# Inputs of a gated encoder layer laid out transposed by the host instead of turned on TensorE

## The chip, the cores and the metric

The kernel runs on one core of one Trainium2 chip. The metric is the device time of one execution in microseconds (us), as the median of repeated runs. The host's work on the inputs is not in it.

## The reference

One layer of an encoder works on x of 256 positions by 2048 channels in float32.

```python
def mixer_block(x, g_norm, w_in, ln_g, ln_b, w_s, b_s, rpb, w_branch, w_out):
    h = rms_norm(x, g_norm)
    proj = h @ w_in                    # 2048 -> 9216: u, v | q, k, v | two gates
    y_a = gmlp_branch(uv, ...)         # u * (W_s LN(gelu(v)) + b), 8 groups of 128 x 128
    y_b = neighbourhood_attn(q, k, v, rpb)
    merged = g_a * (y_a @ w_branch[:1024]) + g_b * (y_b @ w_branch[1024:])
    return x + merged @ w_out

def conv_ffn(x, g_norm, w_up, conv_k, conv_b, w_down):
    up = rms_norm(x, g_norm) @ w_up    # 2048 -> 11008
    ...                                # depthwise conv of width 3 over positions, plus conv_b
    return x + (silu(gate) * val) @ w_down
```

A last RMSNorm ends it. All weights are float32, and nearly all of the time is products with them.

## The kernel before

**Products in parts.** Each float32 operand is split into a high part (rounded, by a ScalarE copy) and a low part (the rest, by a VectorE subtraction), and a product is three matmuls: high by high, low by high, high by low (`triple`, L292 to L294). A matmul moves 512 columns.

**Pieces and groups.** Weights come in pieces of 512 KB: in the wide groups one piece is 128 rows (one k of the 2048-long sum) by 1024 columns. `load_to` issues the loads on SP's queue, up to five pieces ahead (five `wraw` buffers). `split_to` makes `whi` (ScalarE, L152) and `wlo` (VectorE, L153), in four buffers each. `begin(i)` opens piece i: it issues loads, runs the tasks that hand-written tables put at this piece (`at(i, f)`; `preload[i]` for loads that go on SP's queue just ahead of piece i), and splits later pieces. Every engine works through its own queue in this order. Pieces 0 to 15 are the V group (gMLP's v), 16 to 31 the VA group (attention's v), then come U (two groups of eight), q/k with the gates, and the rest.

A plain piece is twelve matmuls. Some pairs of pieces ("quads", at pieces 10 and 12 of V, and 20, 24, 28) save one of eight block products by sums: sums of blocks of x (`act_sums`, L306 and `act_blocks`, L298 to L301), of weights (`weight_sums`, L323 to L326), and splits of these (L313/L314, L333/L334). They need four banks of PSUM beside the four accumulators; there are eight banks.

**x and the vectors.** x is loaded by rows (positions on partitions) into `xs`, 256 columns at a time (`load_x`, 256 KB, L407). For each such chunk `x_chunk` turns four 128 x 128 blocks on TensorE (L510) into a PSUM bank; ScalarE and VectorE make the two parts from there, scaled by the norm vector `gmix` (L482, L489). `X_TURN` says at which piece: chunk 0 ahead of piece 0, chunk 3 at 1, chunks 1 and 4 at 2, 5 at 3, 2 at 4, 6 at 6, 7 at 9. The RMS factor is applied to the results: `x_stats` sums the squares of rows of `xs` on ScalarE (L1195, at pieces 7 to 14), and `x_norm` makes the factor (at 15).

The norm vectors and conv taps are loaded as rows of 128 values and turned on TensorE into columns (`vec_T`, L421, copied by VectorE at L422): `gmix` at the start, `gffn` and the four rows of taps and bias late, at pieces 33 to 35. The spatial weights are loaded into `ws_raw` and turned at pieces 31 and 32 (`turn_ws`, L1223, copied at L1224). TensorE's queue also has transposes of the identity that keep its clock up while the first loads are under way (`keep_awake`, L447): nine ahead of the turned `gmix`, eight after the first chunk of x.

Of the kernel before, what the change touches and what calls it, by code (L numbers as in the profile page):

```python
# [62 lines left out]
@with_exitstack  # L63
def trunk_kernel(ctx, tc, x, norm_mix, w_in, ln_g, ln_b, w_s, b_s, rpb, w_branch, w_out,
                 norm_ffn, w_up, conv_k, conv_b, w_down, norm_final, out):
    nc = tc.nc
# [22 lines left out]
    def bank():  # L89
        return psum.tile([128, 512], F32, name="bank")  # L90
# [19 lines left out]
    n_split = [0]  # L110
    first = {}

# [28 lines left out]
    def split_to(n):  # L141
        while n_split[0] < min(n, len(pieces)):
            i = n_split[0]
            n_split[0] += 1
            src, r0, kn, (c0, cn, nb, cs), step = pieces[i]
            w = raw.pop(i)
            h = wpool.tile([128, 2, 512], F32R, name="whi", bufs=SPLIT_AHEAD + 1)
            l = wpool.tile([128, 2, 512], F32R, name="wlo", bufs=SPLIT_AHEAD + 1)
            m = cn * nb

            def part(k):
                nc.scalar.activation(h[:, k, :m], w[:, k, :m], AF.Copy)  # L152
                nc.vector.tensor_sub(l[:, k, :m], w[:, k, :m], h[:, k, :m].bitcast(F32))  # L153
# [16 lines left out]
    def at(i, f):  # L170
        tasks.setdefault(i, []).append(f)
# [113 lines left out]

    def sum_acts_at(i, j, box, pair, room, name):
        at(i, lambda: act_sums(pair(), box, room))
        at(j, lambda: act_sums_split(box, room, name))
# [13 lines left out]

    def act_sums(a, box, room):
        w = room("f", F32)
        f = w[:, 0].rearrange("p (k t) -> p k t", k=2)
        nc.vector.tensor_add(f, a[:, :, 0, :].bitcast(F32), a[:, :, 1, :].bitcast(F32))  # L306
        act_blocks(w[:, 1], *(f[:, k, t * 128:(t + 1) * 128] for k in range(2) for t in range(2)))
        box["w"] = w
# [101 lines left out]
    def rows(src, off, n):  # L410
        return bass.AP(tensor=src.tensor, offset=src.offset + off, ap=[[128, n], [1, 128]])

    def vec_T(name, src, off, n, dst, queue=None):
        t = xin.tile([n, 128], F32, name=name)

        def load():
            (queue or nc.sync).dma_start(t, rows(src, off, n))

        def go():
            p = bank()  # L420
            nc.tensor.transpose(p[:, :n], t, ident[:n, :n])  # L421
            nc.vector.tensor_copy(dst, p[:, :n])  # L422
        return load, go

    gmix = const.tile([128, KD], F32)
    gffn = const.tile([128, KD], F32)
    ck = const.tile([128, 4, 2 * NF], F32)
    gm_load, gm_turn = vec_T("gm_rows", norm_mix, 0, KD, gmix, nc.scalar)
    gm_load()
    ws_raw = xin.tile([128, GMG, 128], F32)  # L430

    def load_ws():
        nc.sync.dma_start(ws_raw, bass.AP(tensor=w_s.tensor, offset=w_s.offset,
                                          ap=[[128, 128], [128 * 128, GMG], [1, 128]]))

# [12 lines left out]

    keep_awake(WAKE[0])
    late = [vec_T("gf_rows", norm_ffn, 0, KD, gffn)]  # L450
    for j in range(3):
        late.append(vec_T(f"ck_rows{j}", conv_k, j * 2 * DFF, 2 * NF, ck[:, j, :]))
    late.append(vec_T("cb_rows", conv_b, 0, 2 * NF, ck[:, 3, :]))


# [47 lines left out]
    x_pairs = [pair_of[hpool, f"h{c}"] for c in range(KD // 2)]  # L503

    def x_chunk(c):
        p = bank()
        for kk in range(2):
            k = c * 2 + kk
            for t in range(NT):
                nc.tensor.transpose(p[:, kk * T + t * 128:kk * T + (t + 1) * 128],  # L510
                                    xs[:, t, k * 128:(k + 1) * 128], ident)
        split_pair(p, xT[2 * c:2 * c + 2], gmix[:, 2 * c:2 * c + 2])

# [611 lines left out]
    for n, (q, i, j) in enumerate(X_SUMS):  # L1125
        sum_acts_at(i, j, first_sums[2 * q], lambda q=q: x_pairs[q],
                    lambda name, dt, i=i: first_room("s2" if name == "f" and i < 9 else name, dt), f"s{n}")
    g_u = [stationary(w_in2, 0, KD, U0 + j * 512, 512, 1, 0, xt, ev_u(j)) for j in range(2)]
# [73 lines left out]

    for n in range(8):
        at(STATS_AT + n, lambda n=n: x_stats(*divmod(n, 2)))
    at(NORM_AT, x_norm)
# [13 lines left out]

    def turn_ws(h):  # L1220
        p = bank()
        for g in range(4):
            nc.tensor.transpose(p[:, g * 128:(g + 1) * 128], ws_raw[:, h * 4 + g, :], ident)  # L1223
        nc.vector.tensor_copy(gm_pool["wsT"][:, h * 4:h * 4 + 4, :].rearrange("p a b -> p (a b)"), p)  # L1224
# [90 lines left out]
    def load_fin():  # L1315
# [12 lines left out]

_INS = ['x', 'norm_mix', 'w_in', 'gm_ln_g', 'gm_ln_b', 'gm_w_s', 'gm_b_s', 'na_rpb', 'w_branch', 'w_out',
        'norm_ffn', 'w_up', 'conv_k', 'conv_b', 'w_down', 'norm_final']  # L1330
_OUTS = [((1, 256, 2048), 'float32')]
# [23 lines left out]
```

## Time and profile before

| | us |
|---|---|
| median of 3 runs | 1311.91 (1311.79 to 1312.01) |
| the profiled execution, its own time | 1312.27 |
| span of its trace | 1310.5 |
| TensorE busy | 1299.2 (99%) |
| VectorE busy | 1076.5 (82%) |
| ScalarE busy | 774.2 (59%) |
| first product of the V group starts | 6.50 |
| first product of the U group after its last turn starts | 96.05 |

In a line of the timeline the first number is the start in us from the span's start, the second how long it took, then come engine, line of the kernel, operation, tiles (out<-in), shapes, count, and in brackets the idle time of the engine before it and what ended that. PE is TensorE's matmuls, DVE VectorE, ACT ScalarE, SPq the DMA queue of SP, ACTq that of ScalarE. In a line of waits stand the waiting operation, what it waited for, the sum in us, how often, and the longest.

### The profile page before, as it was taken

What the parts mean: (1) busy time and instruction counts of PE and PEld (TensorE: products, weight loads), DVE (VectorE), ACT (ScalarE), POOL (GpSimd) and SP (SyncE); (2) the same over time, 40 slices, a digit from 0 to 9 for tenths busy, and PEclk for the clock granted to TensorE, in tenths of its full rate; (3) what the DMA queues carried; (4) which work ended last, traced back from release to release, by engine and by line L of the source; (5) the groups of instructions that cost most, each with busy time, mean ns of one, the idle gap of its engine ahead of it and who ended that gap; (6) DMA issues with size and microseconds to landing.
All of it is one profiled execution on the core that took longest, in us unless ns stands there. A gap on an engine that the chain in (4) does not pass through costs nothing.

```text
span 1310.5 us, 19358 instructions
## 1 busy us (share of the span) xinstructions
PE 1299.2 (99%) x6758; PEld 1109.4 (85%) x6758; DVE 1076.5 (82%) x1627; ACT 774.2 (59%) x1147; POOL 104.5 (8%) x206
## 2 busy tenths in 40 slices
PE   9999999999999999999999999999999999999997
PEld 7888888888888888888888888888888888888885
DVE  7996777668679966986787878787788879999997
ACT  5766476666645644556655656565565656655563
POOL 0004505323000000000000000000000000000000
PEclk9999999999999999999999999999999999999999
DMA  8768656556556666665656566666666658876882
GB/s 305 257 214 229 204 177 192 183 172 181 187 165 213 201 199 228 214 212 162 192 181 208 182 218 194 213 205 209 185 217 193 212 159 291 287 270 223 270 288 106
DMA packets 174898, 275.11 MB, mean 210 GB/s; under 512 B 13144, under 2 KB 124624, under 8 KB 174800
## 3 DMA queue, kind: packets, MB, share of 16 engines
q1 hardware_dynamic: 166448, 250.31, 59.2%
q0 software_dynamic: 8032, 23.03, 5.7%
q8 instruction: 53, 0.87, 0.3%
q10 hardware_dynamic: 320, 0.53, 0.1%
q14 instruction: 45, 0.37, 0.1%
HBM read 264.38 MB, written 7.34 MB: 207 GB/s over the span
## 4 chain that ended last, share of the span: by engine, by line
PE 98%; DVE 1%; ACT 0%; issue 0%; DMA 0%; ACTq 0%; DVEq 0%
PE bank L206 31%; PE bank L210 16%; PE bank L292 12%; PE bank L293 12%; PE bank L294 12%; PE bank L234 5%; PE bank L236 4%; PE bank L235 4%; PE bank L768 1%; PE bank L818 0%; PE bank L510 0%; PE bank L634 0%; PE bank L808 0%; PE bank L899 0%; PE bank L971 0%
## 5 line engine op out<-in xcount | busy, mean ns | idle before, releaser
L153 DVE TENSOR_TENSOR wlo<-wraw,whi 128x1024 fp32r<-128x1024 f32 (+1 forms) x472 | 546.1, 1171 | 182.3 <-ACT whi L152 98.8
L152 ACT ACTIVATE whi<-wraw 128x1024 fp32r<-128x1024 f32 (+1 forms) x472 | 470.5, 1011 | 219.8 <-PE bank L293 84.9
L206 PE MATMUL bank<-h,whi 128*128 128x512 f32 x1760 | 425.9, 392 | 0.0
L206 PEld LDWEIGHTS bank<-h,whi 128*128 128x128 f32 x1760 | 321.9, 188 | 61.8
L210 PEld LDWEIGHTS bank<-h,wlo 128*128 128x128 f32 x1760 | 225.9, 191 | 8.8
L210 PE MATMUL bank<-h,wlo 128*128 128x256 f32 x1760 | 228.6, 283 | 0.0
L997 ACT ACTIVATE tc<-ta,ck 128x256 f32<-128x256 f32 x86 | 47.1, 594 | 117.1 <-DVE ta L995 117.1
L294 PE MATMUL bank<-wlo,a 128*128 128x512 f32 x224 | 87.3, 390 | 0.0
L293 PE MATMUL bank<-whi,a 128*128 128x512 f32 x224 | 87.2, 389 | 0.0
L292 PE MATMUL bank<-whi,a 128*128 128x512 f32 x224 | 87.1, 389 | 0.0
L292 PE MATMUL bank<-whi,h 128*128 128x512 f32 x210 | 83.0, 395 | 0.0
L294 PE MATMUL bank<-wlo,h 128*128 128x512 f32 x210 | 82.0, 391 | 0.0
L293 PE MATMUL bank<-whi,h 128*128 128x512 f32 x210 | 82.0, 391 | 0.0
L333 ACT ACTIVATE h<-h 128x1024 fp32r<-128x1024 f32 x40 | 40.2, 1053 | 33.8 <-DVE h L325 33.8
L1000 DVE SCALAR_TENSOR_TENSOR tc<-ta,ck,tc 128x255 f32<-128x255 f32 x86 | 41.4, 481 | 14.4 <-ACT tc L997 14.4
L234 PE MATMUL bank<-whi,y 128*128 128x512 f32 x128 | 50.5, 394 | 0.0
L234 PE MATMUL bank<-whi,h 128*128 128x512 f32 x128 | 50.4, 394 | 0.0
L236 PE MATMUL bank<-wlo,h 128*128 128x512 f32 x128 | 49.9, 390 | 0.0
L236 PE MATMUL bank<-wlo,y 128*128 128x512 f32 x128 | 49.9, 390 | 0.0
L235 PE MATMUL bank<-whi,y 128*128 128x512 f32 x128 | 49.8, 389 | 0.0
L235 PE MATMUL bank<-whi,h 128*128 128x512 f32 x128 | 49.8, 389 | 0.0
L294 PEld LDWEIGHTS bank<-wlo,a 128*128 128x128 f32 x224 | 42.0, 188 | 9.1 <-DVE wlo L153 0.3
(300 smaller groups left out, 1801.0 us busy)
## 6 DMA issues: line engine op xcount, KB each, us to landing
wraw<-in_w_up_dram SPq DMA_DIRECT2D x336, 256.0 KB, 3.4
wraw<-in_w_in_dram SPq DMA_DIRECT2D x111, 512.0 KB, 4.4
wraw<-in_w_down_dram SPq DMA_DIRECT2D x86, 512.0 KB, 5.3
wraw<-in_w_in_dram SPq DMA_DIRECT2D x66, 256.0 KB, 3.5
wraw<-in_w_branch_dram SPq DMA_DIRECT2D x32, 512.0 KB, 4.5
wraw<-in_w_out_dram SPq DMA_DIRECT2D x32, 512.0 KB, 4.1
h<-sums POOLq DMA_DIRECT2D x20, 512.0 KB, 6.9
sums<-so POOLq DMA_DIRECT2D x10, 512.0 KB, 4.3
```

The lines of the kernel that those rows point to most:

```text
L152: nc.scalar.activation(h[:, k, :m], w[:, k, :m], AF.Copy)
L153: nc.vector.tensor_sub(l[:, k, :m], w[:, k, :m], h[:, k, :m].bitcast(F32))
L206: nc.tensor.matmul(p, h[:, k - k0, b * 128:(b + 1) * 128], acts(k), start=k == 0, stop=k == nk - 1)
L210: nc.tensor.matmul(p[:, :T], l[:, k - k0, b * 128:(b + 1) * 128], acts(k)[:, 0, :], start=False, stop=False)
L234: nc.tensor.matmul(p, xh, h[:, kk, :m], start=st, stop=False)
L235: nc.tensor.matmul(p, xl, h[:, kk, :m], start=False, stop=False)
L236: nc.tensor.matmul(p, xh, l[:, kk, :m], start=False, stop=sp)
L292: nc.tensor.matmul(p, xh, h, start=st, stop=False)
L293: nc.tensor.matmul(p, xl, h, start=False, stop=False)
L294: nc.tensor.matmul(p, xh, l, start=False, stop=sp)
L997: nc.scalar.activation(v, u, AF.Identity, scale=ck[:, 1, ch:ch + 1], bias=ck[:, 3, ch:ch + 1])
L1000: nc.vector.scalar_tensor_tensor(v[:, 1:], u[:, :T - 1], ck[:, 0, ch:ch + 1], v[:, 1:], op0=OP.mult, op1=OP.add)
```

## The change

The host hands over x a second time, transposed and cut by k (`x_t`, 128 x 16 x 256), all norm and conv vectors as columns in one array (`vecs`, 128 x 376), and the spatial weights transposed (`w_st`).

- `x_chunk` turns nothing: `x_split` makes both parts of one k from `xr`, loaded from `x_t` (256 KB a chunk, in the places of the loads by rows). Chunk 0 comes in two halves, k = 0 on SP's queue and k = 1 on ScalarE's. The first half of piece 0's weights is split after k = 0, then k = 1, then the second half.
- `act_sums` for V and VA makes its sum f by two ScalarE copies from `xr` (scaled by `gmix`) instead of one VectorE addition of the parts.
- `gmix`, `gffn` and the taps are loaded as columns; the six turns and copies fall away. The late ones are two loads, with piece 20 (five with piece 14 before).
- The spatial weights are loaded into `wsT` with piece 30 (`ws_raw` with 13 before); both turns and copies fall away.
- x by rows is still needed for its squares: four loads of 512 KB ahead of pieces 8, 11, 14 and 17. The squares move from pieces 7 to 14 to 7, 8, 10, 11, 13, 14, 15 and 16, the norm from 15 to 17.
- The layer-norm vectors and the spatial bias are loaded with pieces 24, 26 and 28 (21, 16 and 17 before).
- The waking transposes are seventeen in one run at the start.

```diff
-WAKE = (9, 8)
+WAKE = 17
-STATS_AT, NORM_AT, LN_AT, WS_AT, LATE_AT, ATTN_AT = (7, 15, 31, 31, 33, 2)
-LOAD_WS, LOAD_LN, LOAD_LATE = (13, (21, 16, 17), 14)
+STATS_AT, NORM_AT, LN_AT, LATE_AT, ATTN_AT = ((7, 8, 10, 11, 13, 14, 15, 16), 17, 31, 33, 2)
+LOAD_ROWS, LOAD_WS, LOAD_LN, LOAD_LATE = ((8, 11, 14, 17), 30, (24, 26, 28), 20)
...
             else:
                 part(slice(0, 1))
-                first["rest"] = lambda: part(slice(1, 2))
+                x_split(1)
+                part(slice(1, 2))
...
         load_to(i + LOAD_AHEAD)
-        if i == 0:
-            gm_turn()
-            split_to(1)
...
-    def act_sums(a, box, room):
+    def act_sums(a, box, room, early):
         w = room("f", F32)
         f = w[:, 0].rearrange("p (k t) -> p k t", k=2)
-        nc.vector.tensor_add(f, a[:, :, 0, :].bitcast(F32), a[:, :, 1, :].bitcast(F32))
+        if early:
+            for kk in range(2):
+                nc.scalar.activation(f[:, kk], xr[:, 2 * a + kk], AF.Copy, scale=gmix[:, 2 * a + kk:2 * a + kk + 1])
+        else:
+            nc.vector.tensor_add(f, a[:, :, 0, :].bitcast(F32), a[:, :, 1, :].bitcast(F32))
...
+    xr = xin.tile([128, KD, T], F32, name="xr")
...
+    def load_xt(k, n, queue=None):
+        (queue or nc.sync).dma_start(xr[:, k:k + n], x_t[:, k:k + n])
...
-    gm_load, gm_turn = vec_T("gm_rows", norm_mix, 0, KD, gmix, nc.scalar)
-    gm_load()
-    ws_raw = xin.tile([128, GMG, 128], F32)
+    nc.scalar.dma_start(gmix, vecs[:, 0:KD])
+    load_xt(1, 1, nc.scalar)
+
+    def load_late():
+        nc.sync.dma_start(gffn, vecs[:, KD:2 * KD])
+        nc.sync.dma_start(ck.rearrange("p a b -> p (a b)"), vecs[:, 2 * KD:])
 
     def load_ws():
-        nc.sync.dma_start(ws_raw, ...)
+        nc.sync.dma_start(gm_pool["wsT"], w_st)
...
+    def x_split(k):
+        a, g = xT[k], gmix[:, k:k + 1]
+        nc.scalar.activation(a[:, 0, :], xr[:, k], AF.Copy, scale=g)
+        nc.vector.scalar_tensor_tensor(a[:, 1, :], xr[:, k], g, a[:, 0, :].bitcast(F32), op0=OP.mult, op1=OP.subtract)
+
     def x_chunk(c):
-        p = bank()
-        for kk in range(2):
-            k = c * 2 + kk
-            for t in range(NT):
-                nc.tensor.transpose(p[:, kk * T + t * 128:kk * T + (t + 1) * 128],
-                                    xs[:, t, k * 128:(k + 1) * 128], ident)
-        split_pair(p, xT[2 * c:2 * c + 2], gmix[:, 2 * c:2 * c + 2])
+        for k in (2 * c, 2 * c + 1):
+            x_split(k)
...
-    preload[0] = [lambda: load_x(0, 256)]
+    preload[0] = [lambda: load_xt(0, 1)]
     for n, (c, _) in enumerate(X_TURN[1:]):
-        preload[n + 2] = [lambda c=c: load_x(256 * c, 256)]
-    at(0, lambda: x_chunk(0))
-    at(0, lambda: first["rest"]())
-    at(0, lambda: keep_awake(WAKE[1]))
+        preload[n + 2] = [lambda c=c: load_xt(2 * c, 2)]
+    for n, i in enumerate(LOAD_ROWS):
+        preload.setdefault(i, []).append(lambda n=n: load_x(512 * n, 512))
+    at(0, lambda: x_split(0))
+    at(0, lambda: split_to(1))
...
-    def turn_ws(h):
-        ...
-    at(WS_AT, lambda: turn_ws(0))
-    at(WS_AT + 1, lambda: turn_ws(1))
-    preload[LOAD_LATE] = [ld for ld, _ in late]
-    for n, (_, f) in enumerate(late):
-        at(LATE_AT + n // 2, f)
+    preload.setdefault(LOAD_LATE, []).append(load_late)
```

More of the change, by code (lines that the diff above doesn't have):

```diff
@@ L63, in trunk_kernel @@
 @with_exitstack
-def trunk_kernel(ctx, tc, x, norm_mix, w_in, ln_g, ln_b, w_s, b_s, rpb, w_branch, w_out,
-                 norm_ffn, w_up, conv_k, conv_b, w_down, norm_final, out):
+def trunk_kernel(ctx, tc, x, x_t, vecs, w_in, ln_g, ln_b, w_st, b_s, rpb, w_branch, w_out, w_up, w_down,
+                 norm_final, out):
     nc = tc.nc
@@ L110, in trunk_kernel @@
     n_split = [0]
-    first = {}
     def load_to(n):
@@ L284, in wide, with sum_acts_at @@
         return ("wide", n0, order, acts, quads, boxes, done)
-    def sum_acts_at(i, j, box, pair, room, name):
-        at(i, lambda: act_sums(pair(), box, room))
+    def sum_acts_at(i, j, box, pair, room, name, early=False):
+        at(i, lambda: act_sums(pair(), box, room, early))
         at(j, lambda: act_sums_split(box, room, name))
@@ L408, in load_x @@
                           bass.AP(tensor=x.tensor, offset=x.offset + c0, ap=[[D, 128], [128 * D, NT], [1, n]]))
[L410 to L419, printed above, removed]
-            p = bank()
-            nc.tensor.transpose(p[:, :n], t, ident[:n, :n])
-            nc.vector.tensor_copy(dst, p[:, :n])
-        return load, go
+    def load_xt(k, n, queue=None):
+        (queue or nc.sync).dma_start(xr[:, k:k + n], x_t[:, k:k + n])
     gmix = const.tile([128, KD], F32)
@@ L447, in keep_awake @@
             nc.tensor.transpose(wake[:, :128], ident, ident)
[L449 to L453, printed above, removed]
+    keep_awake(WAKE)
     def rstd(name, ssum, n, eps):
@@ L1125, in trunk_kernel @@
     for n, (q, i, j) in enumerate(X_SUMS):
-        sum_acts_at(i, j, first_sums[2 * q], lambda q=q: x_pairs[q],
-                    lambda name, dt, i=i: first_room("s2" if name == "f" and i < 9 else name, dt), f"s{n}")
+        sum_acts_at(i, j, first_sums[2 * q], lambda q=q: q,
+                    lambda name, dt, i=i: first_room("s2" if name == "f" and i < 9 else name, dt), f"s{n}", True)
     g_u = [stationary(w_in2, 0, KD, U0 + j * 512, 512, 1, 0, xt, ev_u(j)) for j in range(2)]
@@ L1201, in x_norm @@
         st1["r"] = r
-    for n in range(8):
-        at(STATS_AT + n, lambda n=n: x_stats(*divmod(n, 2)))
+    for n, i in enumerate(STATS_AT):
+        at(i, lambda n=n: x_stats(*divmod(n, 2)))
     at(NORM_AT, x_norm)
@@ L1218, in trunk_kernel @@
             dst, bass.AP(tensor=src.tensor, offset=src.offset, ap=[[0, 128], [1, GMW]]))]
-    def turn_ws(h):
[L1221 to L1224, printed above, removed]
-    at(WS_AT, lambda: turn_ws(0))
-    at(WS_AT + 1, lambda: turn_ws(1))
-    preload[LOAD_LATE] = [ld for ld, _ in late]
-    for n, (_, f) in enumerate(late):
-        at(LATE_AT + n // 2, f)
+    preload.setdefault(LOAD_LATE, []).append(load_late)
     def open_attn():
@@ L1326, in trunk_kernel @@
     finish_tasks()
-_INS = ['x', 'norm_mix', 'w_in', 'gm_ln_g', 'gm_ln_b', 'gm_w_s', 'gm_b_s', 'na_rpb', 'w_branch', 'w_out',
-        'norm_ffn', 'w_up', 'conv_k', 'conv_b', 'w_down', 'norm_final']
+_INS = ['x', 'x_t', 'vecs', 'w_in', 'gm_ln_g', 'gm_ln_b', 'w_st', 'gm_b_s', 'na_rpb', 'w_branch', 'w_out', 'w_up',
+        'w_down', 'norm_final']
 _OUTS = [((1, 256, 2048), 'float32')]
@@ L1342, with columns @@
     arrays, args = {}, []
+    def columns(name):
+        return _np.asarray(inputs[name]).reshape(-1, 128).T
+    laid = dict(inputs)
+    laid["x_t"] = _np.asarray(inputs["x"])[0].T.reshape(KD, 128, T).transpose(1, 0, 2)
+    laid["vecs"] = _np.concatenate([columns(n) for n in ("norm_mix", "norm_ffn", "conv_k", "conv_b")], axis=1)
+    laid["w_st"] = _np.asarray(inputs["gm_w_s"])[0].transpose(2, 0, 1)
     for name in _INS:
-        a = _np.ascontiguousarray(inputs[name])
+        a = _np.ascontiguousarray(laid[name])
         arrays[f"in_{name}_dram"] = a
```

3 lines of the change are left out of this document (removed).

## The prediction

> **What bounds the kernel now.** I read the page's first part, then what TensorE waited for, then busy time by stretch, then what ScalarE and VectorE waited for while the first two groups run (12 to 92 us), and last the timeline around each edited step.
>
> ```profile
> PE 1299.2 (99%) x6758; PEld 1109.4 (85%) x6758; DVE 1076.5 (82%) x1627; ACT 774.2 (59%) x1147; POOL 104.5 (8%) x206
> ```
>
> The waits of TensorE over the whole span (us in total, times, longest):
>
> ```profile
> PE bank L447 <- POOL ident masks.py:199: 1.4, 1, 1.4
> PE bank L292 <- ACT h L333: 0.6, 1, 0.6
> PE bank L510 <- DMA xs<-in_x_dram: 0.2, 1, 0.2
> ```
>
> After the first product TensorE waits once, for 0.6 us. Whatever takes TensorE time after that costs wall time, so what the change takes off TensorE is worth its price wherever the operands are ready sooner too. That condition is the question. Busy time by stretch (from:to, length, then engines, clock, DMA share, GB/s):
>
> ```profile
> 9.00:18.00 9.00, 9.00 (x49) 7.53 (x48) 7.38 (x14) 5.51 (x12) 0.00 (x0) 1.00 1.05 408
> 30.00:60.00 30.00, 29.40 (x132) 24.04 (x131) 29.39 (x44) 20.56 (x36) 0.61 (x2) 1.00 0.75 258
> 60.00:92.00 32.00, 32.00 (x142) 26.49 (x142) 31.76 (x40) 21.81 (x26) 0.00 (x0) 1.00 0.67 216
> ```
>
> VectorE is busy 29.39 of 30 and 31.76 of 32 us: in the V and VA groups it is as full as TensorE. The DMA engines are full only up to 18 us, at 408 GB/s; then 258 and 216. The waits of ScalarE from 12 to 80 us (first two rows), and all waits of VectorE from 12 to 92 us:
>
> ```profile
> ACT whi L152 <- PE bank L293: 6.5, 4, 2.1
> ACT h L482 <- PE bank L510: 5.5, 3, 3.3
> ```
>
> ```profile
> DVE wlo L153 <- ACT whi L152: 1.4, 1, 1.4
> DVE h L489 <- ACT h L482: 0.4, 1, 0.4
> DVE n_r L463 <- ACT n_s L462: 0.3, 1, 0.3
> ```
>
> ScalarE waits for TensorE, not for a weight load: in this stretch the weights are early.
>
> **The turns of x.** Each of eight chunks takes four transposes, and the first comes before the first product.
>
> ```profile
> L510 PE MATMUL bank<-ident,xs x32: 270/272/474, 4.0 to 35.0; 128*128 128x128 f32 x32
> L1223 PE MATMUL bank<-ident,ws_raw x8: 270/272/273, 92.5 to 96.0; 128*128 128x128 f32 x8
> ```
>
> ```profile
> 9.81 0.39 PE L294 MATMUL bank<-wlo,h 128*128 128x512 f32 x1
> 10.04 0.60 PE L510 MATMUL bank<-ident,xs 128*128 128x128 f32 x4
> 10.40 0.48 PE L292 MATMUL bank<-whi,h 128*128 128x512 f32 x1
> 10.71 0.40 PE L293 MATMUL bank<-whi,h 128*128 128x512 f32 x1
> ```
>
> From 9.81 to 10.71 there are two products and one group of four. Two products alone take 0.46 us at the steady pitch of 0.23 (9.81 to 10.04), so one group costs 0.44. Seven groups after the start: 3.1 us of TensorE. The two of the spatial weights: 0.88.
>
> **The start.**
>
> ```profile
> 4.02 1.11 PE L510 MATMUL bank<-ident,xs 128*128 128x128 f32 x4 [0.19 <-DMA xs<-in_x_dram]
> 4.71 0.63 ACT L152 ACTIVATE whi<-wraw 128x512 fp32r<-128x512 f32 x1 [1.97 <-DMA wraw<-in_w_in_dram]
> 4.93 1.91 PE L447 MATMUL bank<-ident 128*128 128x128 f32 x8
> 5.24 0.82 ACT L482 ACTIVATE h<-bank,gmix 128x256 fp32r<-128x256 f32 x2
> 6.50 0.78 PE L292 MATMUL bank<-whi,h 128*128 128x512 f32 x1
> ```
>
> The first product now comes at 6.50, behind the turns and eight waking transposes. After the change it needs the rounded weights, 4.71 + 0.63 = 5.34, and the rounded x, made from the DMA directly. x chunk 0 had landed by 4.02 as 256 KB; half of it (k = 0) should land earlier, and 0.41 of ScalarE (half of 0.82) follows. So the first product can start at about 5.3, 1.2 sooner. Eight waking transposes filled 4.93 to 6.50, 0.20 each; seventeen from 1.4 (the first wait above) end at about 4.8, before that product. The second half of the chunk (k = 1) comes over ScalarE's queue, behind the norm vector, so issued some 0.5 later than the 256 KB that were there by 4.02: by 4.5 at the latest, before ScalarE reaches it at 5.3. Behind it on ScalarE stands the second half of piece 0, which TensorE wants only after six products.
>
> The norm vector now lands as 128 rows of 64 bytes in place of 16 of 512 that were turned.
>
> ```profile
> 0.75 0.46 ACTq L417 DMA_DIRECT2D gm_rows<-in_norm_mix_dram  x1
> ```
>
> ```profile
> gm_rows<-in_norm_mix_dram ACTq DMA_DIRECT2D x1, 8.0 KB, 2.8
> ```
>
> It was there at 0.75 + 2.8 = 3.55; the first product can bear it 1.4 us later (5.34 - 0.41 - 3.55), so I take nothing. The Trainium skill ("DMA: Bandwidth & Descriptors", Specifications) speaks against this edit: transfers under 512 B are done as read-modify-write and miss line rate. No row here has 64 bytes, so the trace cannot settle it; by that rule the start would slip only if the landing lost over 1.4 us, and the sum below, which does not hang on the start, would stay.
>
> **What the feed gives back.** The start and the five groups up to 20 us sum to 1.2 + 2.2 = 3.4. They are not all kept:
>
> ```profile
> 10.75 1.06 ACT L152 ACTIVATE whi<-wraw 128x1024 fp32r<-128x1024 f32 x1 [1.16 <-DMA wraw<-in_w_in_dram]
> ```
>
> ```profile
> 11.85 1.23 DVE L153 TENSOR_TENSOR wlo<-wraw,whi 128x1024 fp32r<-128x1024 f32 x1 [1.45 <-ACT whi L152]
> ```
>
> ```profile
> 16.48 0.68 DVE L306 TENSOR_TENSOR y<-h 128x512 f32<-128x512 f32 x1
> 17.19 0.29 DVE L298 TENSOR_TENSOR y<-y 128x128 f32<-128x128 f32 x1
> ```
>
> ```profile
> 19.33 1.22 DVE L153 TENSOR_TENSOR wlo<-wraw,whi 128x1024 fp32r<-128x1024 f32 x1
> ```
>
> ```profile
> 20.99 0.39 PE L294 MATMUL bank<-wlo,h 128*128 128x512 f32 x1
> ```
>
> Piece 2 lands at 10.75 (the bytes ahead of it are the same after the change), and from 11.85 VectorE works without a gap up to the low part of piece 4, done at 20.55 and used at 20.99. The change takes one step out of this chain, the sum at L306, now made by two ScalarE copies: 16.48 to 17.19 = 0.71. ScalarE has room for them, since it no longer waits for turns. So the low part of piece 4 is done at 19.84, and its product starts at about 19.95 in place of 20.99: **1.04 kept of 3.4**. TensorE will wait there, and at piece 2, where the x low part stands behind VectorE's split. This is the largest step of the sum.
>
> **After that.** Two more groups of turns, at pieces 6 and 9, fall away: 0.88. Then the one wait of TensorE:
>
> ```profile
> 41.03 0.87 DVE L489 SCALAR_TENSOR_TENSOR h<-bank,gmix,h 128x256 fp32r<-128x256 f32 x2
> ```
>
> ```profile
> 42.05 0.47 PE L292 MATMUL bank<-y,y 128*128 128x512 f32 x1 [0.60 <-ACT h L333]
> ```
>
> The view names ScalarE's L333, but that product's weight sums are y tiles, split earlier. It is the first into the third of four new banks; the four accumulators hold the other four of eight, so one of the new ones is that of x chunk 7, which VectorE reads until 41.90. After the change x holds no bank: 0.6 and the slower first step behind it, together 0.7.
>
> The spatial weights: 0.88. The five late vectors:
>
> ```profile
> 98.53 0.23 PE L421 MATMUL bank<-ident,gf_rows 16*128 16x16 f32 x1
> ```
>
> ```profile
> 98.77 2.11 PE L206 MATMUL bank<-h,whi 128*128 128x512 f32 x8
> ```
>
> ```profile
> 102.61 0.31 PE L421 MATMUL bank<-ident,ck_rows 86*128 86x86 f32 x2
> 102.71 2.10 PE L206 MATMUL bank<-h,whi 128*128 128x512 f32 x8
> 104.65 0.24 PE L421 MATMUL bank<-ident,cb_rows 86*128 86x86 f32 x1
> ```
>
> 0.24 + 0.10 + about 0.03, and 0.08 after each of three stops (10.40 to 10.71 is 0.31 in place of 0.23): 0.6. Their copies on VectorE go with them.
>
> **What is added.** Four loads of x by rows, 524 KB each at 408 GB/s: 1.3 us each, 5.1 in all, ahead of pieces 8, 11, 14 and 17 in SP's order. Hidden: ScalarE waits for no weight there. If that cover were gone they would cost up to 5.1; the bound below is zero. I take 0, nearest to the rows. The squares wait for these rows and keep the weight splits behind them on ScalarE waiting, but each load is issued several pieces ahead. The norm (a reduction, a ScalarE root and five small steps) moves from piece 15 to 17, into VectorE's queue ahead of the low part of piece 21:
>
> ```profile
> 53.54 0.15 DVE L1199 TENSOR_REDUCE ss<-xsq 128x2 f32<-128x8 f32 x1
> ```
>
> ```profile
> 55.04 2.47 DVE L544 TENSOR_TENSOR vg<-bank,vg 128x512 f32<-128x512 f32 x4
> ```
>
> That is 1.5 us from one to the other, which TensorE's lead over VectorE paid at piece 17 without a wait. Bounds 0 and 1.5; taken 0.2, near the row. The late loads on SP become two instead of five, and the layer-norm and spatial loads, with pieces 24 to 30 now, are first read after piece 31: 0.
>
> **Sum:** 1.04 + 0.88 + 0.7 + 0.88 + 0.6 - 0.2 = 3.9, say 4.0. After 110 us nothing is edited and TensorE never waits, so it is carried to the end. The profiled execution took 1312.27 (span 1310.5), 0.36 over the median of 1311.91: 1308.3 there, and 1307.9 as a median.
>
> **Rivals.**
> - *VectorE sets the pace up to 92 us.* For: 29.39 of 30 and 31.76 of 32. Then only the three sums that leave it count, 3 x 0.71, and the late vectors: 2.1 + 0.6 = 2.7, 1309.2. Against: TensorE never waited for VectorE after the start, except as a holder of a bank, so it has some lead to spend.
> - *The feed keeps up.* If the x and weights of pieces 2 to 4 come earlier than I think, all 3.4 stay: 3.9 + 2.4 = 6.3, 1305.6. Against: VectorE's chain from 11.85.
> - *The row loads come on the path (slower).* They stand ahead of four weight pieces in one queue. If pieces 8 to 17 then land after TensorE wants them, 5.1 is paid, what was won before (1.04 + 0.88 + 0.7) is lost, and of the gains only 1.5 stays: 1311.9 + 5.1 - 1.5 = 1315.5. It decides when a piece comes later than the lead; 408 GB/s is reached before 18 us, and pieces and rows together need 7.3 MB in ten pieces of twelve products, 2.7 us each: 270. Against it, strongly.
> - *It does nothing.* Matmul ends are modelled, and the Trainium skill ("Trainium Kernel Development and Optimization", Performance Expectations) calls matmul busy time a bad metric for the distance to the roofline. If the turns ran in time that TensorE had to spare, 1311.9. The pitch speaks against it: products follow at 0.23 on both sides of a group and 0.44 is lost at each.
>
> **How the numbers follow.** Forecast 0.60, VectorE's pace 0.15, feed keeps up 0.08, row loads 0.08, nothing 0.09. 0.2% is 2.6 us, about what a measurement here can tell from no change, so 1309.3 divides. The forecast's own range is 1306.8 to 1309.0; to leave out no more than 2 in 10 I go from 1305.6 (near the full gain) to 1310.8 (VectorE's pace and 1.6 of the row loads). Faster by over 0.2%: the forecast, the full gain and most of VectorE's pace, 0.78; within: 0.14; slower: 0.08.
>
> **What would show it.** First product near 5.3; TensorE waits of about 1 us at piece 2 and 0.6 at piece 4, for VectorE; no wait near 40 us; rows of L510, L1223 and L421 gone; the first U product about 3.4 us sooner; no DMA among ScalarE's waits after 12 us. It is wrong if TensorE waits in VA for more than 0.5, or if a whi split waits for a weight load after 20 us.

## The result and the profile after

| | before | after |
|---|---|---|
| median of eight runs each | 1311.89 (1311.46 to 1312.34) | 1308.29 (1307.79 to 1309.20) |
| the profiled execution | 1312.27 | 1307.83 |
| span of its trace | 1310.5 | 1306.0 |

The ratio of the times is 0.9973, 95% interval 0.9962 to 0.9984: the changed kernel is 3.6 us faster. The profiled execution of the changed kernel is one of its quicker ones; between the two profiled executions the difference is 4.4. Run again beside other kernels (below, `after_again`), it took 1307.88, ratio 0.9969 (0.9956 to 0.9981).

The first part of the page after, and what TensorE waited for over the span (us in total, times, longest):

```profile
PE 1293.6 (99%) x6712; PEld 1103.9 (85%) x6712; DVE 1072.5 (82%) x1616; ACT 776.8 (59%) x1153; POOL 104.7 (8%) x206
```

```profile
PE bank L440 <- POOL ident masks.py:199: 1.4, 1, 1.4
PE bank L290 <- DVE h L496: 0.8, 1, 0.8
PE bank L291 <- DVE wlo L152: 0.7, 2, 0.5
PE bank L289 <- ACT h L495: 0.6, 1, 0.6
```

TensorE has 46 instructions less and is busy 5.6 us less (1299.2 to 1293.6). It now waits 2.1 us after the start (0.8 + 0.7 + 0.6), where before it waited 0.8 (0.6 + 0.2). 5.6 - 2.1 + 0.8 = 4.3, which is the difference of the two profiled executions within 0.2. Busy and idle time make up the span, so this is bookkeeping, but it tells what became of the work: the change took it off TensorE, and a part of what that won turned into waits.

Busy time by stretch (from:to, length, then PE, PEld, DVE, ACT, POOL, clock, DMA share, GB/s):

```profile
9.00:18.00 9.00, 7.65 (x33) 5.77 (x33) 6.50 (x15) 7.63 (x14) 0.00 (x0) 1.00 1.04 417
30.00:60.00 30.00, 30.00 (x134) 24.86 (x133) 29.42 (x43) 21.22 (x36) 0.61 (x2) 1.00 0.78 272
60.00:92.00 32.00, 31.47 (x139) 25.50 (x138) 29.51 (x37) 22.29 (x27) 0.00 (x0) 1.00 0.73 248
```

TensorE has holes where it had none: 1.35 us from 9 to 18, and 0.53 from 60 to 92. From 30 to 60 it lost its hole. VectorE went from 31.76 to 29.51 of 32 in the last stretch: no longer full.

Where the gain comes and goes is read by taking the same product in both timelines. Products of one kind come in the same order in both kernels, so the n-th product of one is the n-th of the other:

| product | before | after | sooner |
|---|---|---|---|
| the first | 6.50 | 5.23 | 1.27 |
| first of piece 2 | 14.05 | 11.85 | 2.20 |
| second of piece 2 | 14.36 | 13.11 | 1.25 |
| third of piece 4 | 20.99 | 19.21 | 1.78 |
| first of piece 6 | 26.38 | 24.33 | 2.05 |
| behind the last turns of x | 37.89 | 35.21 | 2.68 |
| behind the bank wait near 42 us | 52.35 | 48.81 | 3.54 |
| in piece 22 | 72.75 | 70.21 | 2.54 |
| first of U | 96.05 | 92.65 | 3.40 |
| behind the late vectors | 120.35 | 116.08 | 4.27 |
| last of the kernel | 1300.95 | 1296.63 | 4.32 |

Rows of the start after the change: TensorE first, then ScalarE, then VectorE.

```profile
5.23 0.78 PE L289 MATMUL bank<-whi,h 128*128 128x512 f32 x1
5.82 0.42 PE L290 MATMUL bank<-whi,h 128*128 128x512 f32 x1
6.08 0.40 PE L291 MATMUL bank<-wlo,h 128*128 128x512 f32 x1
...
11.85 0.50 PE L289 MATMUL bank<-whi,h 128*128 128x512 f32 x1 [0.59 <-ACT h L495]
13.11 0.50 PE L290 MATMUL bank<-whi,h 128*128 128x512 f32 x1 [0.75 <-DVE h L496]
...
19.21 0.50 PE L291 MATMUL bank<-wlo,h 128*128 128x512 f32 x1 [0.16 <-DVE wlo L152]
```

```profile
10.34 1.06 ACT L151 ACTIVATE whi<-wraw 128x1024 fp32r<-128x1024 f32 x1 [2.44 <-DMA wraw<-in_w_in_dram]
11.30 0.89 ACT L495 ACTIVATE h<-xr,gmix 128x256 fp32r<-128x256 f32 x2
```

```profile
11.43 1.22 DVE L152 TENSOR_TENSOR wlo<-wraw,whi 128x1024 fp32r<-128x1024 f32 x1 [2.73 <-ACT whi L151]
12.57 0.87 DVE L496 SCALAR_TENSOR_TENSOR h<-xr,gmix,h 128x256 fp32r<-128x256 f32 x2
...
17.93 3.50 DVE L152 TENSOR_TENSOR wlo<-wraw,whi 128x1024 fp32r<-128x1024 f32 x3
```

TensorE reaches piece 2 at 11.26 and finds nothing: the weights landed at 10.34 (a wait of ScalarE of 2.44 ends there), then come the rounding, the parts of x behind it, and VectorE's. The 1.27 and the turns that TensorE saved before this point are mostly gone: 2.20 at the first product of piece 2, 1.25 at the second.

The two rows of the DMA issues that bear on the added loads (times, KB each, median us from issue to landing):

```profile
xs<-in_x_dram SPq DMA_DIRECT2D x4, 512.0 KB, 6.3
```

```profile
gmix<-in_vecs_dram ACTq DMA_DIRECT2D x1, 8.0 KB, 2.4
```

### The profile page after: what moved, and what is told of

Same layout as the page of the kernel before. It is cut to its first block, busy times and chain, and to the rows that moved or that the text cites. A ratio compares the mean times of both kernels' runs of the same rounds, so it can differ in the third digit from the quotient of the medians.

```text
span 1306.0 us, 19254 instructions
## 1 busy us (share of the span) xinstructions
PE 1293.6 (99%) x6712; PEld 1103.9 (85%) x6712; DVE 1072.5 (82%) x1616; ACT 776.8 (59%) x1153; POOL 104.7 (8%) x206
## 4 chain that ended last, share of the span: by engine, by line
PE 96%; DVE 1%; ACT 1%; DMA 1%; issue 0%; SPq 0%; ACTq 0%; DVEq 0%
PE bank L203 31%; PE bank L207 16%; PE bank L291 11%; PE bank L289 11%; PE bank L290 11%; PE bank L231 5%; PE bank L233 4%; PE bank L232 4%; DMA wraw<-in_w_in_dram 1%; PE bank L756 1%; PE bank L806 0%; DVE wlo L152 0%; PE bank L622 0%; PE bank L796 0%; PE bank L887 0%
```

## The experiments

Each was timed in five rounds beside the kernel before, which took 1311.9 to 1312.0 us each time. Times are the medians, with the lowest and the highest in brackets. "Gain" is how much sooner than in the trace of before a product comes.

### The changed kernel once more, and the norm put back

`after_again` has no edit.

> The changed kernel once more, as the measure for the runs beside it. All theories: about 3.6 us below the kernel before, a span of about 1306.0, and in the trace waits of TensorE at piece 2 (0.6 and 0.75), piece 4 (0.2) and piece 22 (0.5). If the time now hangs on when the first weight pieces land, its runs spread more than those of the kernel before (1.4 us against 0.9 so far).

Measured: 1307.88 (1307.24 to 1308.80). The waits stand at the same places (0.65 at piece 2, 0.14 at piece 4, 0.53 at piece 22), only that the first product of piece 2 no longer waits. The gain at the end of its trace is 4.6.

`e_norm` puts the squares and the norm back to the pieces where they stood before, and the loads of the rows closer together to fit:

```
-STATS_AT, NORM_AT, ... = ((7, 8, 10, 11, 13, 14, 15, 16), 17, ...)
+STATS_AT, NORM_AT, ... = ((7, 8, 9, 10, 11, 12, 13, 14), 15, ...)
-LOAD_ROWS, ... = ((8, 11, 14, 17), ...)
+LOAD_ROWS, ... = ((8, 10, 12, 14), ...)
```

> The changed kernel with the norm back at piece 15, the squares at pieces 7 to 14, and the four row loads at pieces 8, 10, 12 and 14. Theory: the wait at piece 22 comes from the norm at 17, whose ScalarE root waits for VectorE (ScalarE idle from 53.5 to 57.8 in the changed kernel) and holds the weight splits behind it. Then ScalarE's wait of 4.3 us is gone, TensorE does not wait at piece 22, and the first U product comes 1.0 us sooner than in the changed kernel: span about 1305.0. Rival: VectorE is full up to 92 us whatever the place of the norm: the wait of 0.5 stays, span 1306.0. Second rival: the row loads, now closer together, make a weight piece late: a ScalarE wait for a weight load before 50 us, and up to 1.3 us lost.

Measured: 1308.85 (1307.78 to 1309.11), ratio 0.9974 (0.9963 to 0.9985). What TensorE waited for:

```profile
PE bank L203 <- DVE ya L626: 0.8, 1, 0.8
...
PE bank L291 <- DVE wlo L152: 0.5, 1, 0.5
```

The 0.5 at piece 22 stays as it was (at 67.03). My theory that the moved norm makes this wait fell. The first of these rows is new: at 141.10 a product of the next group waits 0.84 for a bank that VectorE's fourth mix add holds. In this execution it takes 1.1 of the gain (4.38 ahead of it, 3.26 behind it).

### The sums of x

Before, VectorE made each of the three sums f of x in one add. After, ScalarE makes each in two copies. `e_f` gives all three back to VectorE, `e_third` only the last one, at piece 18:

```
-    sum_acts_at(i, j, ..., lambda q=q: q, ..., f"s{n}", True)
+    sum_acts_at(i, j, ..., lambda q=q: x_pairs[q], ..., f"s{n}")                                   # e_f
+    sum_acts_at(i, j, ..., lambda q=q, n=n: q if n < 2 else x_pairs[q], ..., f"s{n}", n < 2)       # e_third
```

> The changed kernel with the sums f of V and VA made by one VectorE addition again, in place of two ScalarE copies. Theory: VectorE's chain from piece 2 sets piece 4, so the addition's 0.71 comes back there: the wait at piece 4 grows from 0.2 to about 0.9; the wait at piece 22, behind two more additions, is not smaller: span 1306.7 to 1307. Rival: the feed is set by loads or ScalarE, which has 0.8 less to do for each sum: span 1306.0 or less.

Measured: 1307.83 (1307.19 to 1308.37). TensorE's waits:

```profile
PE bank L291 <- DVE wlo L152: 0.9, 1, 0.9
PE bank L290 <- DVE h L496: 0.8, 1, 0.8
PE bank L203 <- DVE ya L626: 0.2, 1, 0.2
```

The 0.9 is at piece 4 (19.61), where the changed kernel waits 0.16. Nothing is left at piece 22: the gain is 3.01 at 52 us and 2.84 at 80, where it is 3.54 and 2.54 after the change. So the first of the three sums is rightly on ScalarE and the third is not, and in the sum over all three the two nearly cancel. The second was not tried alone. The trace of the changed kernel shows how the third does harm. ScalarE, then VectorE, then TensorE:

```profile
58.88 1.99 ACT L334 ACTIVATE y<-y 128x1024 fp32r<-128x1024 f32 x2
61.41 0.91 ACT L305 ACTIVATE y<-xr,gmix 128x256 f32<-128x256 f32 x2 [0.53 <-DVE y L335]
62.34 1.28 ACT L548 ACT_TABLE_LOAD   x1
63.63 1.15 ACT L548 ACTIVATE vg<-vg,n_r 128x1024 f32<-128x1024 f32 x1
...
64.78 1.04 ACT L151 ACTIVATE whi<-wraw 128x1024 fp32r<-128x1024 f32 x1
```

```profile
65.86 1.22 DVE L152 TENSOR_TENSOR wlo<-wraw,whi 128x1024 fp32r<-128x1024 f32 x1 [2.29 <-ACT whi L151]
```

```profile
66.21 0.40 PE L290 MATMUL bank<-whi,h 128*128 128x512 f32 x1
67.13 0.50 PE L291 MATMUL bank<-wlo,h 128*128 128x512 f32 x1 [0.53 <-DVE wlo L152]
67.47 0.40 PE L289 MATMUL bank<-whi,h 128*128 128x512 f32 x1
```

The two copies (L305) write a tile that VectorE's L335 still reads, so ScalarE stands 0.53, and behind the copies are the gelu's table load, the gelu and then the split of piece 22. VectorE is idle 2.29 for that split, and TensorE at last 0.53. It costs 1.0 (3.54 to 2.54), and the rows show how. From 66.21 to 67.13 are 0.92 in place of the pitch of 0.23, a loss of 0.69: the idle time is counted from the end of the product before, but the next would have started 0.17 ahead of that end. The step behind the wait is 0.34, 0.11 too long, and the two ahead of it are 0.07 and 0.10 too long.

> The third sum of x (f of piece 18) is added by VectorE as before the change; the first two stay ScalarE's copies. Theory (those two copies queue behind VectorE's y at about 61 us and push the gelu table load and with it the first split of piece 22 late): ScalarE goes from y straight to the table load, TensorE's wait of 0.53 at 67 us is gone and the product after piece 22 gains about 3.5 us on the kernel before and not 2.54; the end comes 1.0 sooner, a span near 305.0 above 1000, 1306.9 as a time, unless it is paid back at about 140 us, where VectorE's fourth mix add releases a bank. Rival (VectorE itself is full at piece 20 to 22, and the add on it costs what ScalarE's copies cost): the wait stays at 0.5, the time is the changed kernel's 1307.9.

Measured: 1306.81 (1306.22 to 1309.10), ratio 0.9962 (0.9950 to 0.9975). ScalarE goes from the sums' split straight to the table load:

```profile
58.24 1.99 ACT L334 ACTIVATE y<-y 128x1024 fp32r<-128x1024 f32 x2
60.25 1.28 ACT L548 ACT_TABLE_LOAD   x1
61.55 1.15 ACT L548 ACTIVATE vg<-vg,n_r 128x1024 f32<-128x1024 f32 x1
...
62.70 1.04 ACT L151 ACTIVATE whi<-wraw 128x1024 fp32r<-128x1024 f32 x1
```

TensorE does not wait at 67 us; the gain is 4.20 at 52 us and 4.20 at 80, and 5.9 at the end. So the 1.0 is shown and is not paid back later: of the 1.6 between the gains at the end (5.94 and 4.32) 1.0 is this wait, and 0.65 came earlier (2.70 and 2.05 at piece 6), from pieces that landed sooner in this execution (next part). The intervals of the two times overlap; it is the trace that tells the kernels apart.

### The start

`e_order` splits piece 2 later in ScalarE's and VectorE's queues, so that x stands ahead of it; `e_wake` has eight waking transposes less; `e_defer` (which also has the edits of `e_best2`, below) loads and splits chunk 1 of x behind chunks 4 and 5, whose loads move up, so its split comes two pieces later (chunk 2's, and the first sum of x, one piece later):

```
-SPLIT_TO = (3, 4, 4, ...)                                       # e_order
+SPLIT_TO = (2, 4, 4, ...)
-WAKE = 17                                                       # e_wake
+WAKE = 9
-X_TURN = ((0, 0), (3, 1), (1, 2), (4, 2), (5, 3), (2, 4), ...)  # e_defer
+X_TURN = ((0, 0), (3, 1), (4, 2), (5, 3), (1, 4), (2, 5), ...)
-X_SUMS = ((1, 3, 4), ...)
+X_SUMS = ((1, 4, 5), ...)
```

> The changed kernel with piece 2 split after the x chunk that it multiplies, not ahead of it. Theory: at piece 2 TensorE waits for the low part of x, which stands behind the weight split on VectorE, while VectorE was idle from 8.7 to 11.4 and x had landed at 9.1. Then the second product of piece 2 no longer waits, the third comes at about 12.7 in place of 13.4, VectorE's chain up to piece 4 is 0.8 shorter, so that no wait takes its place there: 0.7 us sooner, span about 1305.3. Rival: the landing of piece 2 at 10.3 sets what follows, and the wait moves to the low part of its weights or to piece 4: within 0.2 of the changed kernel.

Measured: 1307.60 (1307.00 to 1308.44). The wait moved to the third product of piece 2 (0.53) and to piece 4 (0.69). TensorE's wait over the span, and the rows of ScalarE that explain it:

```profile
PE bank L291 <- DVE wlo L152: 1.8, 3, 0.7
```

```profile
10.63 1.06 ACT L151 ACTIVATE whi<-wraw 128x1024 fp32r<-128x1024 f32 x1 [0.34 <-DMA wraw<-in_w_in_dram]
12.53 1.06 ACT L151 ACTIVATE whi<-wraw 128x1024 fp32r<-128x1024 f32 x1 [0.84 <-DMA wraw<-in_w_in_dram]
```

Piece 3 lands at 12.53 with ScalarE waiting. VectorE, which has x behind it by then, waits 0.68 for that split. So the rival was right: the landings of pieces 2 and 3 set the start, and work of VectorE that moves ahead of them wins nothing.

> The changed kernel with nine waking transposes in place of seventeen. Theory: the start is not on the path, since TensorE waits at piece 2 anyway: the clock comes up later, pieces 0 and 1 take longer, the wait at piece 2 shrinks from 1.3 towards 0.8, and the product that ended that wait starts at 13.1 as before: span within 0.2 of 1306.0. Rival: the earlier full clock (5.85 in place of 8.02) is part of the gain: pieces 0 and 1 end so late that the second product of piece 2 starts 1 to 2 us later, span 1307 to 1308.

Measured: 1307.67 (1307.44 to 1308.81).

```profile
5.45 0.80 PE L289 MATMUL bank<-whi,h 128*128 128x512 f32 x1 [1.90 <-ACT whi L151]
6.04 0.63 PE L290 MATMUL bank<-whi,h 128*128 128x512 f32 x1
...
8.18 0.47 PE L289 MATMUL bank<-whi,h 128*128 128x512 f32 x1
8.48 0.40 PE L290 MATMUL bank<-whi,h 128*128 128x512 f32 x1
...
13.13 0.50 PE L290 MATMUL bank<-whi,h 128*128 128x512 f32 x1 [0.36 <-DVE h L496]
```

Products follow each other at 0.43 up to 8.2 (at 0.23 from 6.08 on in the changed kernel), and yet the second product of piece 2 comes at 13.13 as against 13.11. About a microsecond of slow products at the start costs nothing, since TensorE is ahead of the feed there.

> As the last, and the second chunk of x is loaded and split one piece later, behind the third and the fourth piece of weights. Theory (the landings of pieces 2 and 3 and VectorE's queue set the start): piece 3 lands about 0.65 sooner (12.2 to 11.5 us), VectorE's queue up to piece 4 is about 2 us shorter, the waits at pieces 2 and 4 (0.65 and 0.15) shrink to 0.3 in all, and the gain at piece 6 rises from 2.05 to 2.4 to 2.7: time 1306.4 to 1306.7. Rival (the start is bound by the landing of piece 2 alone, which has not moved, and the products follow the feed): the gain at piece 6 stays at 2.0 to 2.1, and the time is that of the last.

Measured: 1306.96 (1306.66 to 1307.80), 0.5 above the kernel without this edit, whose interval it overlaps. Piece 3 landed no sooner relative to piece 2 (12.00 and 10.11): the load of chunk 4 stands ahead of it in the place of chunk 1's, so the edit took no bytes from there. That part of the expectation was wrong. To see the rest, one number ties all executions together: from the start of ScalarE's split of piece 2 (its landing) to the first product of piece 6.

| run | piece 2 split from | first of piece 6 | between |
|---|---|---|---|
| before | 10.75 | 26.38 | 15.63 |
| after | 10.34 | 24.33 | 13.99 |
| after_again | 9.99 | 23.98 | 13.99 |
| e_norm | 10.29 | 24.33 | 14.04 |
| e_wake | 10.36 | 24.35 | 13.99 |
| e_rows | 10.06 | 24.06 | 14.00 |
| e_mix | 10.34 | 24.37 | 14.03 |
| e_third | 9.68 | 23.67 | 13.99 |
| e_best2 | 9.51 | 23.50 | 13.99 |
| e_f | 10.00 | 24.72 | 14.72 |
| e_order | 10.63 | 24.59 | 13.96 |
| e_defer | 10.13 | 23.68 | 13.55 |

In the eight executions with the changed kernel's start (`e_wake`'s with fewer waking transposes) the distance is 13.99 to 14.04, while the landing scatters by 0.85 us. The start is the landing of piece 2 plus a fixed chain behind it. From the landing of piece 3, 1.9 later, to piece 4 that chain is VectorE's: one add more on it (`e_f`) makes it 0.73 longer. `e_order` took VectorE's work out ahead of that landing, and the distance stayed. `e_defer` took a pair of x parts and a sum out behind it, so that VectorE comes to piece 4 1.84 sooner after the landing of piece 2; of this 0.44 is kept, since TensorE no longer waits at piece 4 and has nothing more to win there. What `e_defer` won it lost at 41.06, where TensorE waits 0.44 for the low part of a piece, at a cost of 0.75.

### The other parts, one by one

`e_bank` is the kernel before with the last chunk of x turned at piece 7 instead of 9; `e_consts` is the kernel before with only the vectors and the spatial weights laid out by the host; `e_rows` is the changed kernel without the loads by rows, with its squares taken of the transposed x, so that it leaves out the layer's true norm:

```
-X_TURN = (..., (6, 6), (7, 9))        # e_bank
+X_TURN = (..., (6, 6), (7, 7))
-    at(WS_AT, lambda: turn_ws(0))      # e_consts: and gm_turn, vec_T, as in the change
-        preload.setdefault(i, []).append(lambda n=n: load_x(512 * n, 512))    # e_rows:
+        pass                                                                 # squares of xr
```

> The kernel before with x chunk 7 turned at piece 7 in place of 9, two pieces sooner, nothing else. Theory: the one wait of TensorE at 42 us is for the PSUM bank of that chunk, which VectorE reads until 41.9: it goes away, and all after it is 0.7 us sooner: span about 1309.8. Rival: it is the wait for ScalarE's sums that the view names (L333): it stays at about 0.6, span 1310.5.

Measured: 1311.21 (1310.88 to 1312.03), ratio 0.9995 (0.9986 to 1.0004), which includes 1, so the trace has to tell. The wait near 42 is gone from the view:

```profile
PE bank L447 <- POOL ident masks.py:199: 1.4, 1, 1.4
PE bank L510 <- DMA xs<-in_x_dram: 0.2, 1, 0.2
```

The gain rises there from 0.29 to 1.15, that is by 0.86. No work was taken away, only the bank came free sooner. ScalarE's L333 ran from 39.95 to 41.96 before and from 40.45 to 42.46 here, later, and yet the product starts at 41.00, ahead of its end. So the wait that the view put down to L333 was one for a bank, as the prediction said.

> The kernel before with the vectors and the spatial weights laid out by the host, loaded in their old places, and x still loaded by rows and turned on TensorE. Theory: this part is worth its TensorE time, 0.88 for the spatial weights and 0.6 to 0.8 for the late vectors, and nothing at the start, as the first chunk of x is turned ahead of the first product anyway: 1.5 to 1.7 us, span about 1308.9, and the rest of the change (x) is the larger part, 2.7. Rival: its copies off VectorE, or the start without the turned norm vector, free more: over 2.5.

Measured: 1309.93 (1309.63 to 1311.71), ratio 0.9986 (0.9977 to 0.9995). Its wait near 42 stays:

```profile
PE bank L291 <- ACT h L332: 0.6, 1, 0.6
```

Its gain is 0.48 up to 92 us, 1.46 behind the place of the spatial turns and 2.2 behind that of the late vectors, where it stays. The edited places are thus worth 1.7, as the theory had it. The 0.48 is from the start, and `e_bank`, whose start is that of the kernel before, has 0.29 there too, so at least a part of it is no effect of the edit. Of the 3.6 some 1.7 to 2.0 are the vectors and the spatial weights, and the rest is x.

> The changed kernel without the four row loads; the squares are taken of the transposed x that is there already, so the norm of the first stage is wrong and the work on ScalarE the same. Theory: the row loads are hidden: span within 0.2 of 1306.0. Rival: they delay the weight pieces behind them in SP's queue, 1.3 us each: up to 5 us less, and weight pieces that TensorE takes sooner.

Measured: 1308.80 (1307.72 to 1310.56), ratio 0.9977 (0.9967 to 0.9986). Without the 2.1 MB of rows it is not faster: from piece 6 to the end of its trace the gain rises by 2.2 (2.32 to 4.50), with them by 2.3 (2.05 to 4.32). The rows are hidden; the rival that put them on the path is refuted.

### Two versions further

`e_mix` puts VectorE's adds of the mixed vectors one piece sooner; `e_best2` is this and the edit of `e_third`:

```
-                at(i + 3 + b, lambda g=j * 4 + b: mix(g))
+                at(i + 2 + b, lambda g=j * 4 + b: mix(g))
```

> VectorE's adds of the mixed vectors stand one piece sooner in the first stage's order, all else as changed. Theory (some executions of the changed kernel lose about 1 us at 140 us, where a bank of the next group waits for the fourth of these adds, and that makes the spread of its times, 1307.2 to 1309.2): the fourth add ends about 5 us sooner than 139.7, TensorE never waits for it, the runs spread by 0.9 or less and the median is 1307.5 or a little less. Rival (the spread is made at the start by the landing of the first pieces): the times keep their spread of 1.2 to 2 us about 1307.9. If the weights of the mix land too late for it, TensorE waits newly before 140 us and the time is 1308.5 or more.

Measured: 1307.65 (1307.38 to 1308.02). TensorE does not wait near 140, but it did not in the changed kernel's own trace either. The fourth add ended 0.25 us sooner, not 5: this stretch waits for weights, and VectorE, whichever order it has, stands behind the splits.

```profile
127.01 1.23 DVE L152 TENSOR_TENSOR wlo<-wraw,whi 128x1024 fp32r<-128x1024 f32 x1 [2.38 <-ACT whi L151]
```

So the edit hardly tested the theory. That its five times lie within 0.64 could be chance, since `e_best2` has the same edit and scatters again.

> Both: the third sum on VectorE and the adds of the mixed vectors one piece sooner. By the theory the 1.0 us at piece 22 is not paid back at 140 us: span 1305.0, time 1307.0 with a spread under 1. By the rival of the first the wait at 67 us stays and the time is 1307.9; by the rival of the second the median is 1307 with a spread of 1.2 or more.

Measured: 1306.49 (1305.90 to 1308.09), ratio 0.9962 (0.9948 to 0.9975); TensorE does not wait at 67. It is the quickest of all, 5.4 under the kernel before. 1.4 to 1.8 lie between it and the changed kernel's two medians; of this the 1.0 of `e_third`'s edit is shown and nothing more. Its times spread by 2.2, as the second rival had it, so the adds do not make the spread.

## Why the prediction was right

The time of 1307.9 came out as 1308.29, and the sum of 3.9, taken as 4.0, as 3.6 in the medians and 4.4 in the profiled pair. The steps, by the table of products:

- **The start**, predicted 5.3: measured 5.23. (The second half of chunk 0 landed at 4.69 and not by 4.5, still ahead of ScalarE, which came to it at 5.08.) That it would not be kept was right as well, and `e_wake` shows it by its reverse.
- **Kept up to piece 4**, predicted 1.04: measured 1.78. The mechanism was right (VectorE's chain behind the landing of piece 2), its size was not. Three terms make the 1.78. Piece 2 was split from 10.34 and not 10.75, 0.41 sooner; I had it unmoved because the bytes ahead of it were the same. This part may be chance: the three executions with the loads by rows split it from 10.45 (`e_consts`) to 10.75, the eleven with the changed loads from 9.51 to 10.63. The chain from VectorE's first split to the end of piece 4's low part is 7.7 long (11.43 to 17.93 + 1.22), where it was 8.7 (11.85 to 20.55); I had taken 0.71 off. The rest are two short stops of VectorE for ScalarE, which came late behind the turns: the steps at 18.05 and 18.38 took 0.33 and 0.95 before and take 0.21 and 0.79 now. The prediction had VectorE working without a gap there. (The 0.4 in its list of waits stood at 27.53, behind this chain.) Last, TensorE follows this part 0.06 behind, where before it came 0.44 behind and I had let it come 0.11 behind.
- **The two later turn groups**, predicted 0.88: 2.68 - 1.78 = 0.90.
- **The bank wait**, predicted 0.7: 3.54 - 2.68 = 0.86, and `e_bank` gives the same 0.86 alone. The mechanism was right; the step that goes with a wait of 0.60 is larger than the 0.1 that I added (last section).
- **VectorE and ScalarE from piece 16 on**, predicted -0.2, for the norm: measured -1.00, at piece 22. Both the size and the cause were wrong. The norm's move made no wait (`e_norm`). The failing step is "ScalarE has room for them" of the sums' copies: true on the average of the stage, and true at piece 3, where I had looked. At piece 18 the copies stand in line behind a tile that VectorE still reads, and ahead of a table load, a gelu and a split for which VectorE, and through it TensorE, is waiting.
- **The spatial weights**, predicted 0.88: 3.40 - 2.54 = 0.86 at the first U product, 0.97 four products later (97.07 and 93.56), when the slow one behind the turns is past.
- **The late vectors**, predicted 0.6: 4.27 - 3.51 = 0.76.
- **The rows**, predicted 0: none shown (`e_rows` is no faster without them).

Up to U the steps were predicted at 3.3 and measured 3.40, because +0.74 at the start and -0.80 at piece 22 cancelled. That the sum is so near is this luck. One reading was off without weight in the sum: the DMA engines were full up to 20 us and not 18 (401 GB/s from 18 to 20).

Of the marks, first product, no wait near 40, missing turns and first U product came as told. At piece 2 the waits are 0.59 + 0.75 for about 1, and the first of them is for ScalarE's part of x. At piece 4 it is 0.16 and not 0.6. Two marks that would have called it wrong were set off: TensorE waits 0.53 at piece 22, and ScalarE does wait for weights after 20 us:

```profile
76.93 1.06 ACT L151 ACTIVATE whi<-wraw 128x1024 fp32r<-128x1024 f32 x1 [1.06 <-DMA wraw<-in_w_in_dram]
85.87 1.06 ACT L151 ACTIVATE whi<-wraw 128x1024 fp32r<-128x1024 f32 x1 [0.74 <-DMA wraw<-in_w_in_dram]
```

TensorE does not wait behind either, so that mark was wrongly chosen: a wait one engine away from the bottleneck is no cost until the bottleneck waits too. `e_rows` has such a wait of 1.9 as well, so the rows do not make it.

The rivals: *VectorE's pace* is out: with VectorE busy 29.42 of 30 us from 30 to 60 the gain rose by 1.49 between piece 6 and 52 us, and where the third sum went back to VectorE (`e_third`) all of it was kept to 80 us. *The feed keeps up* is out at piece 2. *It does nothing* is out: the time fell, and the interval of the ratio excludes 1. TensorE's busy time fell by 5.6 and the time of the profiled pair by 4.4, so busy time alone would have overstated the gain by the 1.3 that came back as waits. The Trainium skill ("Trainium Kernel Development and Optimization", Performance Expectations), quoted with that rival, calls matmul busy time a bad metric for how close a kernel is to the roofline. That closeness was not measured here. On the other rule weighed there, the Trainium skill ("DMA: Bandwidth & Descriptors", Specifications) says that transfers under 512 B are done as read-modify-write. The norm vector in 128 rows of 64 bytes took 2.4 us from issue to landing in the changed kernel and 2.8 in `e_consts`, the 16 rows of 512 bytes 2.8 before. At 8 KB, here, the rule shows no price.

**What stays open.** The changed kernel's times scatter by 1.4 to 1.6 us, those of before by 0.9 to 2.1. The landing of piece 2 scatters by 0.85 between executions and goes into the end one to one as far as piece 6, and two executions paid 0.2 and 0.84 at 140 us for a bank. These two could make the changed kernel's scatter, but no run shows it: only profiled executions have a trace. Nor is it shown that the changed kernel scatters more than that of before. Why piece 2 lands sooner after the change, and by how much in each execution, was not found.

## What to carry to other kernels

Follow one product through both timelines. The n-th product's gain, written down at eleven places, shows each cost and where it is paid, and it found both wrong terms here, which cancelled in the total. When work moves to an engine that is 60% busy, look at what stands behind it in that engine's queue at every place where it is put, and at whose tile it writes: the same two copies won 0.7 at piece 3 and lost 1.0 at piece 18. A start bound by landings is a fixed chain behind them, and only work that stands behind the last landing in the chain counts; work taken off an engine that waits there anyway (turns, waking) comes back as waiting.

## What the runs showed of the hardware

- TensorE's products went from a pitch of 0.43 to 0.23 at 8.2 us in the kernel before and in `e_wake`, and from the third product, 6.08 us, in the changed kernel. The pitch follows the granted clock: its record in the trace reaches full speed at 8.03 us before, 8.32 in `e_wake` and 5.85 in the changed kernel. Where it is there before the first product, as in `e_norm`, only the first three steps are long (0.33 to 0.40). The moment scatters between executions: it is 6.91 in `after_again`, the same kernel, 4.68 in `e_norm` with the same start, and 6.25 in `e_bank` with the start of the kernel before. So these runs do not tell how much of `e_wake`'s delay is due to its fewer transposes.
- A wait of TensorE costs 0.26 to 0.31 us more than the idle time that the profile shows: 0.22 (`e_f`, 140 us), 0.44 (`e_defer`, 41 us), 0.53 (changed kernel, 67 us), 0.60 (before, 42 us) and 0.84 (`e_norm`, 141 us) cost 0.50, 0.75, 0.83, 0.86 and 1.12. The products overlap by 0.17 (0.40 long at a pitch of 0.23), which an idle stretch undoes, and the step behind the wait is some 0.1 longer. The 1.0 at 67 us has two late products ahead of the wait as well.
- The same loads, issued at the same time, landed up to 0.85 us apart between executions (piece 2: 9.51 to 10.36 in the eight with the changed kernel's start).
